# Expert tokens fetched from DRAM by row index, two pairs ahead, and RWKV units cut in three, in a two-layer hybrid network

## Chip, cores and metric

The kernel runs on one core of a Trainium2 chip: TensorE (PE) with its weight loads (PEld), VectorE (DVE), ScalarE (ACT), GpSimd (POOL), and SyncE (SP), whose queue issues nearly all transfers. The metric is the device time of one run in microseconds; the runs are of the whole program, both layers and the final norm.

## What is computed

Two streams of 256 tokens each, "latent" and "context", with 1024 channels go through two layers. A layer is a norm, one input projection, four token mixers of 256 channels (RWKV-7 and gated linear attention, both in two directions; window attention; S5), a gated sum of the four branches (the "merge"), an output projection, a second norm, and a mixture of 32 experts with 512 hidden channels. Layer 1 gives out only the latent stream. What the change touches is the experts and the RWKV mixer:

```python
def hier_moe(h, p):                       # n rows of 1024
    g_sel = argmax(hf @ p['w_router_g'] + p['b_router_g'])       # one of 4 groups
    e_logits = (hf @ p['w_router_e'] + ...)[rows, g_sel]         # its 8 experts
    top_v, top_i = lax.top_k(e_logits, TOP_K)                    # TOP_K = 2
    weights = softmax(top_v) * g_w[:, None]
...
    xb = h_pad[buf_tok].reshape(n_blk, MOE_BLOCK, d)             # rows sorted by expert
    def expert_block(args):
        x_blk, e = args
        hid = silu(x_blk @ p['w_exp_gate'][e]) * (x_blk @ p['w_exp_up'][e])
        return hid @ p['w_exp_down'][e]
    y_buf = lax.map(expert_block, (xb, blk_e)).reshape(cap, d) * buf_w[:, None]
    return segment_sum(y_buf, buf_tok, num_segments=n + 1)[:n]
```

The RWKV mixer is a linear recurrence over each stream, forwards and backwards, with a state of 64 x 64 per head; it is computed in chunks of 64 tokens, for which a triangular system is solved in each chunk.

## The kernel before

**Order of the work.** The program text gives the operations in one order; a scheduler places each in its engine's row by when its operands are due, and engines then run their own rows strictly in order. Layer 0 has 512 tokens in four tiles of 128 (`nt` = 4, `lo` = 0), layer 1 256 in two (`nt` = 2, `lo` = 256).

**RWKV units** (`rwkv_units`, L365). A layer has eight units: two halves of the channels (`hf`), two directions (`d`), two streams (`s`). `rwkv_sub` (L464) is one unit: it builds the tiles `ar`, `x`, `bk` and `sm` from decay and keys; writes the 16 x 16 diagonal blocks to DRAM (`ad`), reads them back in another layout (`lt`), solves them on VectorE in 15 steps of two small operations (`tm<-lt,ti`, `ti<-ti,tm`), and sends the inverses through DRAM (`td`) to `dc`; from these come `dT` and the state matmuls (psd, psw, pst, psta), which need the state of the unit before. `rwkv_pre` and `rwkv_half` prepare a direction and a half, `rwkv_finish` (L410) norms a half. Between these matmuls lie those of the merges: eight columns for each of four branches, 24 matmuls of 128x512 (128x256 in layer 1) a column (`pa<-hh,gs`, `pa<-hl,gs`).

**Second norm and routing** (`tail`, L1603). `norm2` norms a tile of 128 tokens to `h2` and, at its end, splits it in three bf16 parts `h2p` (24 KB of each partition in layer 0). `route` finds for each token and expert a position `posm` among that expert's tokens and the weight.

**Experts** (`moe`, L1642; `pair`, L1530). Sixteen pairs of experts, P0 to P15, 64 rows for each expert of a pair. A pair makes one-hot matrices `oh` of 128 tokens x 128 rows, and gathers with them on TensorE: `pg<-oh,h2p`, 8 blocks of channels x `nt` tiles x 3 parts, 96 bf16 matmuls in layer 0, 48 in layer 1, copied to `xT`. It transposes `oh` (pT, `oT`), gets the weights of the rows (pw, `ws`), multiplies gate and up (pgate and pup, 32 matmuls each), makes `hd` of them, transposes that (ph, `hT`), multiplies down (pd, 32), scales by `ws` in two parts `yp`, and puts the rows back to their tokens by matmul (`py<-yp,oT`, 4 x `nt`). Half of the py tiles are scaled and added to `x` by VectorE (`tm`), half by ScalarE and GpSimd (`ta`, three buffers). The gather of a later pair was placed by the scheduler among the matmuls of an earlier one.

**Weights.** A pair needs twelve loads of 1 MB, issued on SP's queue by `wtile` (L224) into a ring of slots: `EB` gives for each layer the tiles on the left and right side; with the four slots of the output projection's weights there are 13 in layer 0 and 15 in layer 1. A load waits for its slot to be read by TensorE's matmuls of the pair before.

A last loop (`overflow`) for experts with over 64 tokens runs no times with these inputs.

Of the kernel before, what the change touches and what calls it, by code (L numbers as in the profile page):

```python
# [9 lines left out]
F32 = mybir.dt.float32  # L10
# [10 lines left out]
D = 1024  # L21
# [3 lines left out]
EB = ((4, 5), (6, 5))  # L25
# [15 lines left out]
C_END = C_ROPE + 128  # L41
# [6 lines left out]
def _consts():  # L48
    c = np.zeros((128, C_END), np.float32)
    p = np.arange(128)  # L50
    c[:, C_ID:C_ID + 128] = np.eye(128)
    s = p % 64
    t = np.arange(64)
    c[:, C_MRW:C_MRW + 64] = s[:, None] < t
    c[:, C_MRW + 64:C_MRW + 128] = s[:, None] <= t
    c[:, C_MG:C_MG + 64] = s[:, None] <= t
    c[:, C_MG + 64:C_MG + 128] = s[:, None] >= t
    q = np.arange(128)
    c[:, C_MA:C_MA + 128] = np.where(q[None, :] <= p[:, None], 0.0, NEG)
# [10 lines left out]
    c[:, C_SEL:C_SEL + 12 * L] = r[:, None] == np.arange(12 * L)  # L70
    c[:, C_SLT:C_SLT + 128] = p[:, None] < p[None, :]
# [104 lines left out]
class Net:  # L176
# [186 lines left out]
    def rwkv_units(self, l, st, yT, p0, pool, depth):  # L363
        self.unit_tiles(st, p0, pool, depth)
        half, pre, sub, fin = self.rwkv_half, self.rwkv_pre, self.rwkv_sub, self.rwkv_finish  # L365
        na, u = st["first"]
        pp = st["pool"]
        for hf in range(2):
            y, nx = yT[:, hf, :], na
            for d in range(2):  # L370
                S = None
                for s in range(2):
                    if d and s and hf == 0:
                        nx = half(l, 1, st, pp)
                    S = sub(hf, d, s, u, S, st, na, y, pool)
                if d == 0:
                    u = pre(hf, 1, st, pp)
                elif hf == 0:
                    u = pre(1, 0, st, pp)
            fin(l, hf, st, y, pool)  # L380
            na = nx
# [28 lines left out]
    def rwkv_finish(self, l, hf, st, y, pool):  # L410
# [5 lines left out]
        ps = self.pc()  # L416
# [3 lines left out]
        s2 = st["pool"].tile([128, 512], F32, tag="pi", name="s2")[:, 0:nlo]  # L420
        self.act(s2, yc, AF.Square)
        ps = self.pc()
# [4 lines left out]
        ps = self.pc()  # L427
# [3 lines left out]
        ps = self.pc()  # L431
# [32 lines left out]
    def rwkv_sub(self, hf, d, s, u, S0, st, na, y, pool):  # L464

        nc = self.nc
        V, G = nc.vector, nc.gpsimd
        self.bt = f"B{s}"
        r, k_, v, lo = st["r"], st["k"], st["v"], st["lo"]
        pp, fo = u  # L470
        pp = pp[:, 4 * s:4 * s + 4, :]
        ident = self.ident
# [34 lines left out]
        ad = self.dr.tile([4, 2, 2, 32, 32], F32, name="ad", tag="ad", bufs=3)  # L507
# [5 lines left out]
        lt = st["p0"].tile([128, 16, 32], F32, tag="lt", bufs=2, name="lt")  # L513
        src = ad.rearrange("j e h s t -> (j e h) (s t)")
        dst = lt.rearrange("p s t -> p (s t)")
        for h in range(2):
            nc.sync.dma_start(dst[64 * h:64 * h + 64, 0:496],
                              src[:, None, 528 * h:528 * h + 496].to_broadcast([16, 4, 496]))
        ti = st["p0"].tile([128, 4, 16], F32, tag="ti", bufs=2, name="ti")
        V.tensor_copy(ti, self.cst[:, C_UN:C_UN + 64].rearrange("p (c t) -> p c t", c=4))  # L520
        tm = st["p0"].tile([128, 4, 16], F32, tag="tm", bufs=2, name="tm")
        for t in range(15):
            n = 15 - t
            self.tt(tm[:, :, 0:n], lt[:, None, t, t + 1:16].to_broadcast([128, 4, n]),
                    ti[:, :, t:t + 1].to_broadcast([128, 4, n]), OP.mult)
            self.tt(ti[:, :, t + 1:16], ti[:, :, t + 1:16], tm[:, :, 0:n], OP.add)
        td = self.dr.tile([128, 64], F32, name="td", tag="td", bufs=3)
        tv = td.rearrange("(q h g) f -> h q g f", h=2, g=4)
        for h in range(2):
            nc.sync.dma_start(tv[h], ti[64 * h:64 * h + 64].rearrange("p c t -> p (c t)"))  # L530
        dc = st["p0"].tile([128, 4, 16], F32, tag="dc", bufs=2, name="dc")
        nc.sync.dma_start(dc, td.rearrange("(j g) (c t) -> (g c) j t", j=4, t=16))
# [880 lines left out]
    def norm2(self, t, x, rw, lo, h2p, wr, lg, pool):  # L1413

        nc = self.nc
        V, G = nc.vector, nc.gpsimd
# [19 lines left out]
        self.split3([h2p[:, i, tl, :] for i in range(3)], h2, V)  # L1436
# [93 lines left out]
    def pair(self, wts, posv, wtv, h2p, x, mb, lo, pool, pooled=(1, 1, 1, 1)):  # L1530

        nc = self.nc
        V, G = nc.vector, nc.gpsimd
        nt = (512 - lo) // 128
        wg, wu, wd = wts
        p = self.onehot(posv, nt, pool, "oh", 2)
        pf = p.rearrange("p t e n -> p t (e n)")
        xT = pool.tile([128, 8, 128], F32, tag="xT", bufs=2, name="xT")
# [13 lines left out]
        V.tensor_copy(oT.rearrange("p t n -> p (t n)"), pT[:, 0:128 * nt])  # L1552
        pw = self.pc("pw")
        for t in range(nt):
            self.mm(pw[:, 0:6], pf[:, t, :], wtv[:, t], t == 0, t == nt - 1)
        ws = pool.tile([128, 1], F32, tag="ws", bufs=2, name="ws")
        for e in range(2):
            r = slice(64 * e, 64 * e + 64)
            V.tensor_reduce(ws[r], pw[r, 3 * e:3 * e + 3], AX.X, OP.add)
# [9 lines left out]
        self.tt(hd, hd, pu, OP.mult)  # L1569
# [15 lines left out]
        for n in range(2):  # L1585
            cs = slice(512 * n, 512 * n + 512)
            for t in range(nt):
# [10 lines left out]
                else:  # L1598
                    tm = pool.tile([128, 512], F32, tag="tm", bufs=2, name="tm")
                    self.tt(tm, ps, mb[s][:, cs], OP.mult)  # L1600
                    self.tt(xo, xo, tm, OP.add)

    def tail(self, l, lo, acc, rm, w):  # L1603
# [7 lines left out]
        st["h2p"] = h2p = rm.tile([128, 3, nt, D], BF, name="h2p")  # L1611
# [4 lines left out]
        with self.tc.tile_pool(name=f"rt{l}", bufs=1, reuse_waits="tile") as rp:  # L1616
# [13 lines left out]
            for t in range(lo // 128, 4):  # L1630
                self.project(t, w, acc, x, bs, lo, rp)
                self.norm2(t, x, rw, lo, h2p, wr, lg, rp)
# [9 lines left out]
    def moe(self, l, lo, st):  # L1642
        nc, io, x = self.nc, self.io, self.x
        posm, wt3, h2p, mb, plan, base = (st[n] for n in ("posm", "wt3", "h2p", "mb", "plan", "base"))
        banks = self.psum(f"pm{l}", G=2, A=2, B=2, C=2)
        self.bt = "B"
        with self.tc.tile_pool(name=f"ep{l}", bufs=1, reuse_waits="tile") as ep:
            for q in range(16):
                e0 = 2 * q
                wg, wu, wd = [[self.blocks([self.eload(l, 12 * q + 4 * i + 2 * h + e) for h in range(2)])  # L1650
                               for e in range(2)] for i in range(3)]
                posv = [posm[:, :, e0 + e:e0 + e + 1] for e in range(2)]
                wtv = wt3[:, :, e0:e0 + 2, :].rearrange("p t e i -> p t (e i)")
# [53 lines left out]
    def overflow(self, l, x, mb, lo, posm, wt3, plan, base, h2p, pool):  # L1707
# [7 lines left out]
        with tc.For_i(0, nv, 1) as b:  # L1715
# [16 lines left out]
            self.pair(w, [pe[:, i] for i in range(2)], wv.rearrange("p t e i -> p t (e i)"), h2p, x, mb, lo, pool)  # L1732
# [174 lines left out]
```

## Time and profile before

| | us |
|---|---|
| runs, lowest / median / highest of three | 2526.41 / 2531.51 / 2534.54 |
| the profiled execution | 2508.66 |
| its span | 2506.9 |
| TensorE busy | 2329.0 (93%) |
| VectorE busy | 1202.6 (48%) |
| ScalarE busy | 670.5 (27%) |
| GpSimd busy | 278.0 (11%) |
| gathers, `pg<-oh,h2p` x2304 | 163.2 busy |
| expert stage, layer 0 / layer 1 | 811 to 1401 / 2000 to 2496 |
| RWKV units, layer 0 / layer 1 | 341 to 585 / 1660 to 1895 |

The profile is of one execution. Busy times are of the engine's whole row; a stage's limits are read from the windows of that stage and from the waits that end last there. A row of the order of time gives start, duration, engine, line, operation, what is written and read, shapes and count; in brackets the idle time before it and what ended that.

### The profile page before, as it was taken

The numbers are of one execution on the slowest core, as the hardware profiler recorded it, in microseconds if no ns is written. First come the engines' busy times: TensorE is split into PE (matmuls) and PEld (weight loads), VectorE is DVE, ScalarE is ACT, GpSimd is POOL, SyncE is SP. The second block draws the span as 40 slices with busy tenths as digits, with TensorE's granted clock in tenths as the row PEclk, the third lists the DMA queues.
The fourth block names the chain that finished last, engine by engine and source line by source line (L and its number), as shares of the span: only waits on it lengthen the run. The fifth ranks groups of instructions, "written<-read, shape, count | busy, mean of one in ns | idle before, by whom it ended". The sixth has DMA issues, their size and how long they took to land. (4 is left out here: it accounts for less than half of the span.)

```text
span 2506.9 us, 42482 instructions
## 1 busy us (share of the span) xinstructions
PE 2329.0 (93%) x17303; PEld 1397.5 (56%) x17303; DVE 1202.6 (48%) x3267; ACT 670.5 (27%) x1229; POOL 278.0 (11%) x305
## 2 busy tenths in 40 slices
PE   5999999999998999999999799989899899999996
PEld 4867666677754445444443576767788444333332
DVE  6686666664435333222223678867665432222222
ACT  3254532323212111111111335543323211111111
POOL 0001000000000133132233100100000011111111
PEclk8999999999998999999999899989999899999999
DMA  6343021215723898787887254412227499999993
GB/s 242 121 146 95 29 64 45 73 43 191 263 70 151 339 389 339 309 334 309 350 315 319 74 169 148 131 56 56 90 63 281 154 417 418 401 397 396 396 409 157
DMA packets 143692, 548.23 MB, mean 219 GB/s; under 512 B 35028, under 2 KB 66132, under 8 KB 93060
## 3 DMA queue, kind: packets, MB, share of 16 engines
q1 hardware_dynamic: 138224, 539.51, 56.9%
q10 hardware_dynamic: 5268, 5.94, 0.7%
q8 instruction: 140, 2.29, 0.4%
q14 instruction: 60, 0.49, 0.1%
HBM read 541.78 MB, written 3.60 MB: 218 GB/s over the span
## 5 line engine op out<-in xcount | busy, mean ns | idle before, releaser
L270 PE MATMUL pa<-hh,gs 128*128 128x512 f32 (+2 forms) x1440 | 421.2, 366 | 10.2 <-ACT sg L273 6.1
L270 PEld LDWEIGHTS pa<-hh,gs 128*128 128x128 f32 (+1 forms) x1440 | 252.4, 188 | 69.8 <-issue 15.3
L270 PE MATMUL pd<-w,hT 128*64 128x512 f32 x1024 | 276.6, 599 | 13.1 <-ACT hT L273 12.4
L270 PE MATMUL pa<-hl,gs 128*128 128x512 f32 (+2 forms) x720 | 252.8, 363 | 0.0
L270 PE MATMUL pgate<-w,xT 128*64 128x512 f32 x1024 | 251.3, 596 | 0.0
L270 PE MATMUL pup<-w,xT 128*64 128x512 f32 x1024 | 249.2, 594 | 0.0
L276 POOL TENSOR_TENSOR ta<-ta,mb 128x512 f32<-128x512 f32 x93 | 127.1, 1373 | 1098.2 <-ACT ta L273 1098.2
L270 PEld LDWEIGHTS <-h2p 128*128 128x128 bf16 x2304 | 134.9, 99 | 78.0 <-issue 72.8
L270 PE MATMUL pg<-oh,h2p 128*128 128x128 bf16 x2304 | 163.2, 223 | 5.8 <-DVE nv L1686 4.2
L276 DVE TENSOR_TENSOR gs<-g,gs 128x1024 fp32r<-128x1024 f32 (+1 forms) x106 | 128.1, 1211 | 83.2 <-PE pa L270 56.7
L270 PEld LDWEIGHTS pd<-w,hT 128*64 128x64 f32 x1024 | 81.5, 136 | 146.7 <-issue 124.3
L273 ACT ACTIVATE gs<-g 128x1024 fp32r<-128x1024 f32 (+1 forms) x106 | 110.5, 1045 | 180.7 <-PE pa L270 139.1
L270 PEld LDWEIGHTS pup<-w,xT 128*64 128x64 f32 x1024 | 78.4, 137 | 143.1 <-issue 138.9
L270 PEld LDWEIGHTS pgate<-w,xT 128*64 128x64 f32 x1024 | 74.8, 137 | 139.6 <-issue 129.4
L270 PEld LDWEIGHTS pa<-hl,gs 128*128 128x128 f32 (+1 forms) x720 | 137.1, 190 | 27.3 <-issue 9.1
L270 PE MATMUL py<-yp,oT 128*128 128x512 f32 x384 | 133.1, 441 | 11.2 <-ACT ta L273 5.5
L286 DVE SCALAR_TENSOR_TENSOR hd<-hd,pgate 128x512 f32<-128x512 f32 x32 | 22.0, 688 | 246.7 <-ACT hd L273 246.7
L276 DVE TENSOR_TENSOR hd<-hd,pup 128x512 f32<-128x512 f32 x32 | 22.0, 688 | 218.0 <-PE pup L270 218.0
L276 POOL TENSOR_TENSOR x<-x,ta 128x512 f32<-128x512 f32 x93 | 122.7, 1326 | 4.9
L286 DVE SCALAR_TENSOR_TENSOR yp<-pd,ws,yp 128x512 fp32r<-128x512 f32 x64 | 47.8, 747 | 152.6 <-ACT yp L273 152.6
L273 ACT ACTIVATE yp<-pd,ws 128x512 fp32r<-128x512 f32 x64 | 44.1, 688 | 272.9 <-PE pd L270 272.9
L276 DVE TENSOR_TENSOR tm<-py,mb 128x512 f32<-128x512 f32 x99 | 66.7, 687 | 95.7 <-PE py L270 95.7
(499 smaller groups left out, 3427.1 us busy)
## 6 DMA issues: line engine op xcount, KB each, us to landing
w<-in_w_g SPq DMA_DIRECT2D x128, 1024.0 KB, 7.9
w<-in_w_d SPq DMA_DIRECT2D x128, 1024.0 KB, 10.5
w<-in_w_u SPq DMA_DIRECT2D x128, 1024.0 KB, 8.6
g<-in_w_ada SPq DMA_DIRECT2D x96, 512.0 KB, 4.0
g<-in_w_in_gate SPq DMA_DIRECT2D x64, 512.0 KB, 3.8
g<-in_w_in_rwkv SPq DMA_DIRECT2D x16, 512.0 KB, 3.6
wb<-in_w_branch SPq DMA_DIRECT2D x64, 128.0 KB, 3.1
w<-in_w_out SPq DMA_DIRECT2D x8, 1024.0 KB, 9.3
```

Source lines behind the costliest of these rows:

```text
L270: self.nc.tensor.matmul(out, lhsT, rhs, start=start, stop=stop, skip_group_check=True)
L273: self.nc.scalar.activation(out, in_, f, **kw)
L276: (eng or self.nc.vector).tensor_tensor(out, a, b, op)
L286: self.nc.vector.scalar_tensor_tensor(out, a, s, b, op0=op0, op1=op1)
```

## The change

The change has three parts.

1. **Experts.** `norm2` no longer splits `h2`; it writes it to DRAM (`h2d`, one transfer on SP for each tile). `pair` is cut: `seek(q)` makes the one-hot matrices, multiplies them with a column of token indices (`tid`) and with the weights (pw), turns the index into an integer (`ix`; rows without a token get one out of bounds) and issues on GpSimd's queue an indirect DMA that takes up to 128 rows of 4 KB from `h2d` to one of three buffers `xg`; rows out of bounds are skipped. `bring(q)` multiplies `xg` by 1 or 0 for rows with or without a token on VectorE, transposes it in eight fp32 blocks on TensorE, copies to `xT`, and makes `oT`. `seek` runs two pairs ahead, `bring` one; `bring`'s multiply is placed behind the pair's last `hd`. At a layer's start three memsets clear `xg`.
2. **Slots.** Two more in layer 0 (15), one more in layer 1 (16).
3. **RWKV units.** `rwkv_sub` becomes `rwkv_head`, `rwkv_solve` and `rwkv_rest`. In layer 0 (`depth` 3) head and solve go three units ahead of rest. In layer 1 (`depth` 4) one solve takes both streams' units: 4 solves of 30 VectorE operations instead of 8, each twice as wide. `rwkv_finish` uses another bank and a tile of its own.

```diff
-EB = ((4, 5), (6, 5))
+EB = ((4, 7), (7, 5))
...
+        nc.sync.dma_start(h2d[128 * tl:128 * tl + 128], h2)
...
-        self.split3([h2p[:, i, tl, :] for i in range(3)], h2, V)
...
+    def seek(self, posv, wtv, h2d, lo, pool):
...
+        p = self.onehot(posv, nt, pool, "oh", 3)
+        pf = p.rearrange("p t e n -> p t (e n)")
+        pw = self.pc("pw")
+        for t in range(nt):
+            self.mm(pw[:, 8:11], pf[:, t, :], self.tid[:, t], t == 0, t == nt - 1)
+        for t in range(nt):
+            self.mm(pw[:, 0:6], pf[:, t, :], wtv[:, t], t == 0, t == nt - 1)
...
+        V.tensor_copy(at[:, 0:3], pw[:, 8:11])
+        self.stt(ix, at[:, 0:1], 1024.0, at[:, 1:2], OP.add, OP.add)
...
+        nc.gpsimd.indirect_dma_start(xg, None, h2d, bass.IndirectOffsetOnAxis(ap=ix, axis=0),
+                                     bounds_check=128 * nt - 1, oob_is_err=False)
+    def bring(self, sent, lo, pool, after=None):
...
+        with self.tc.issue_after(after) if after is not None else nullcontext():
+            self.tsc(xg, xg, at[:, 2:3], OP.mult)
...
-                for t in range(nt):
-                    for i in range(3):
-                        self.mm(ps[:, 128 * kk:128 * kk + 128], h2p[:, i, t, 128 * k:128 * k + 128], pf[:, t, :],
-                                t == 0 and i == 0, t == nt - 1 and i == 2)
+                nc.tensor.transpose(ps[:, 128 * kk:128 * kk + 128], xg[:, 128 * k:128 * k + 128], self.ident)
...
+            sent = seek(0), seek(1)
+            got = self.bring(sent[0], lo, ep)
             for q in range(16):
...
+                sent = sent[1], seek(q + 2)
+                last = self.pair((wg, wu, wd), got, x, mb, lo, ep, (1, q < 15, 1, q < 15))
+                if q < 15:
+                    got = self.bring(sent[0], lo, ep, last)
```

```diff
+        if depth == 4:
+            cur = [head(0, s) for s in range(2)]
+            solve(cur)
+            ahead(1)
+            nxt = [head(1, s) for s in range(2)]
+            for i in range(4):
+                rest(cur[0])
+                if i < 3:
+                    solve(nxt)
+                rest(cur[1])
...
+        else:
...
+            go(0)
+            go(1)
+            ahead(1)
+            go(2)
+            for n in range(8):
+                rest(un[n])
+                if n in (1, 3):
+                    ahead(n // 2 + 2)
+                if n + 3 < 8:
+                    go(n + 3)
```

How the rows move, at three places (names: left of the arrow what is written, right what is read; buffer numbers behind an underscore).

TensorE in layer 0's experts, a late pair before, from the first gate matmul on; `h2p` is the stationary side of the gather:

```order
L270 MATMUL pgate<-w,xT 64x512
L270 MATMUL py<-yp,oT 128x512 x2
L270 LDWEIGHTS h2p
L270 MATMUL pg<-oh,h2p 128x128
...
L270 MATMUL py<-yp,oT 128x512 x4
...
L270 MATMUL pgate<-w,xT 64x512 x15
...
L270 MATMUL pup<-w,xT 64x512
```

The same place in the changed kernel, to the end of the pair:

```order
L272 MATMUL pgate<-w,xT 64x512
L272 MATMUL py<-yp,oT 128x512 x12
L272 MATMUL pgate<-w,xT 64x512 x15
L272 MATMUL pup<-w,xT 64x512 x16
L1663 MATMUL ph<-cst,hd 128x128 x4
...
L1635 MATMUL pg<-cst,xg_7792 128x128 x5
L272 MATMUL pd<-w,hT 64x512 x2
L1635 MATMUL pg<-cst,xg_7792 128x128 x2
L272 MATMUL pd<-w,hT 64x512 x7
L1635 MATMUL pg<-cst,xg_7792 128x128
...
L272 MATMUL pw<-tid,oh 128x3
```

The 96 gather matmuls between py, gate, up and down are gone; eight transposes of `xg` for the next pair, and the small matmuls with `tid` and the weights for a later one, stand behind ph and inside pd.

GpSimd in a late pair of layer 0's experts in the changed kernel; before, the row has the scalings and adds alone:

```order
L278 TENSOR_TENSOR ta<-ta,mb_7647 128x512
L278 TENSOR_TENSOR x_7263<-x_7263,ta 128x512
L278 TENSOR_TENSOR ta<-ta,mb_7647 128x512
L1619 DMA xg_7791<-h2d_7294,ix 128x1024
L278 TENSOR_TENSOR x_7265<-x_7265,ta 128x512
L278 TENSOR_TENSOR ta<-ta,mb_7656 128x512 x2
L278 TENSOR_TENSOR x_7267<-x_7267,ta 128x512
```

The indirect DMA stands between the second tile's scaling and its add, with two more tiles of the pair behind it.

VectorE in layer 1's RWKV units, at the start of a solve, before and in the changed kernel:

```order
L276 TENSOR_TENSOR tm<-lt,ti 128x4x15
L276 TENSOR_TENSOR ar_15166<-na,pp 128x4x64
L276 TENSOR_TENSOR ti<-ti,tm 128x4x15
L283 TENSOR_SCALAR sw<-ic,sp 128x512
L276 TENSOR_TENSOR tm<-lt,ti 128x4x14
```

```order
L278 TENSOR_TENSOR tm<-lt,ti 128x8x15
L278 TENSOR_TENSOR ic<-ic,pi 128x512
L278 TENSOR_TENSOR ti<-ti,tm 128x8x15
L278 TENSOR_TENSOR bk<-kv,sw 64x4x64
L278 TENSOR_TENSOR tm<-lt,ti 128x8x14
```

The steps still alternate with operations of the next units' heads, and each covers two units.

## Rows read from the trace of the kernel before

**Rows 1.** Windows: us, busy us (x instructions) by engine, clock, DMA share, GB/s.
```profile
990.00:1330.00 340.00, 327.98 (x2010) 143.99 (x2007) 79.44 (x142) 53.21 (x89) 90.13 (x70) 1.00 0.82 324
2010.00:2450.00 440.00, 422.54 (x2310) 169.76 (x2306) 102.20 (x189) 69.28 (x114) 73.76 (x56) 1.00 0.99 405
```

**Rows 2.** Waits of SyncE's queue, 990 to 1330 us: total us, times, longest.
```profile
SPq L224 <- PE pgate L270: 119.7, 33, 11.2
```

**Rows 3.** Order of time, TensorE, layer 0: start, us, engine, line, operation.
```profile
811.87 7.20 PE L270 MATMUL pg<-oh,h2p 128*128 128x128 bf16 x96 [2.31 <-DVE nv L1686]
...
819.30 3.23 PE L270 MATMUL pgate<-w,xT 128*64 128x512 f32 x14
...
851.62 7.09 PE L270 MATMUL pgate<-w,xT 128*64 128x512 f32 x32
```

**Rows 4.** Order of time, TensorE, layer 0, P8 and P9.
```profile
1100.76 1.07 PE L270 MATMUL pgate<-w,xT 128*64 128x512 f32 x2
...
1115.82 3.02 PE L270 MATMUL pg<-oh,h2p 128*128 128x128 bf16 x51
...
1141.31 1.07 PE L270 MATMUL pgate<-w,xT 128*64 128x512 f32 x2
```

**Rows 5.** Order of time, TensorE, layer 0, P14 and P15; idle time before in brackets.
```profile
1330.45 1.07 PE L270 MATMUL pgate<-w,xT 128*64 128x512 f32 x2
...
1332.70 1.40 PE L270 MATMUL py<-yp,oT 128*128 128x512 f32 x4 [0.51 <-DVE tm L276]
1334.84 1.19 PE L270 MATMUL py<-yp,oT 128*128 128x512 f32 x4 [0.75 <-ACT ta L273]
...
1351.72 0.66 PE L1572 MATMUL ph<-cst,hd 128*128 128x128 f32 x4 [0.78 <-DVE hd L276]
1352.21 0.39 PE L1550 MATMUL pT<-identb,oh 128*128 128x128 bf16 x4
1353.06 1.93 PE L270 MATMUL pd<-w,hT 128*64 128x512 f32 x4 [0.46 <-ACT hT L273]
...
1363.25 1.07 PE L270 MATMUL pgate<-w,xT 128*64 128x512 f32 x2
```

**Rows 6.** Order of time, TensorE, layer 1: P0, P1, P6, P7, P14, P15.
```profile
2000.42 7.09 PE L270 MATMUL pgate<-w,xT 128*64 128x512 f32 x32
...
2027.71 7.09 PE L270 MATMUL pgate<-w,xT 128*64 128x512 f32 x32
...
2179.70 1.07 PE L270 MATMUL pgate<-w,xT 128*64 128x512 f32 x2
...
2211.45 1.07 PE L270 MATMUL pgate<-w,xT 128*64 128x512 f32 x2
...
2433.04 1.07 PE L270 MATMUL pgate<-w,xT 128*64 128x512 f32 x2
...
2462.38 1.07 PE L270 MATMUL pgate<-w,xT 128*64 128x512 f32 x2
```

**Rows 7.** Order of time, VectorE, routing of layer 0.
```profile
803.86 1.23 DVE L276 TENSOR_TENSOR h2p<-h,h2p 128x1024 bf16<-128x1024 f32 x1 [0.63 <-ACT h2p L273]
```

**Rows 8.** Order of time, GpSimd, layer 0, P14.
```profile
1334.87 1.29 POOL L276 TENSOR_TENSOR ta<-ta,mb 128x512 f32<-128x512 f32 x1 [24.57 <-ACT ta L273]
1336.24 1.60 POOL L276 TENSOR_TENSOR x<-x,ta 128x512 f32<-128x512 f32 x1
```

**Rows 9.** Operations on tile xn: ns min/median/max, first and last start.
```profile
L281 DVE TENSOR_SCALAR xn<-x,n x2: 753/754/754, 1418.0 to 1418.7; 128x1024 f32<-128x1024 f32 x2
```

**Rows 10.** DMA issues: count, KB each, median us to landing.
```profile
out<-o SPq DMA_DIRECT2D x2, 512.0 KB, 2.6
```

**Rows 11.** Waits of TensorE, 341 to 585 us.
```profile
PE psc L270 <- DVE bk L276: 2.9, 2, 2.0
PE pc L270 <- DVE s L286: 2.2, 2, 1.9
```

**Rows 12.** Waits of TensorE, 1660 to 1895 us.
```profile
PE psc L270 <- DVE bk L276: 5.2, 3, 2.2
...
PE pc L270 <- ACT sq L273: 2.7, 1, 2.7
```

**Rows 13.** Windows, RWKV units of layer 1.
```profile
1660.00:1895.00 235.00, 221.92 (x2539) 175.48 (x2540) 159.32 (x534) 75.96 (x150) 1.82 (x5) 0.93 0.27 77
```

More of the change, by code (lines that the diff above doesn't have):

```diff
@@ L1 @@
 import math
-from contextlib import ExitStack
+from contextlib import ExitStack, nullcontext
 import numpy as np
@@ L364, in rwkv_units @@
         self.unit_tiles(st, p0, pool, depth)
-        half, pre, sub, fin = self.rwkv_half, self.rwkv_pre, self.rwkv_sub, self.rwkv_finish
+        pp = st["pool"]
+        sides = [(hf, d) for hf in range(2) for d in range(2)]
         na, u = st["first"]
[L367 to L381, printed above, removed]
+        nas, us, S = {0: na}, {(0, 0): u}, [None]
@@ new lines, in ahead, with solve, rest, head @@
+        def ahead(i):
+            hf, d = sides[i]
+            if hf not in nas:
+                nas[hf] = self.rwkv_half(l, hf, st, pp)
+            us[hf, d] = self.rwkv_pre(hf, d, st, pp)
+        def solve(v):
+            self.rwkv_solve(v, st)
+        def rest(w):
+            hf, d, s = w["at"]
+            S[0] = self.rwkv_rest(w, None if s == 0 else S[0], st, yT[:, hf, :], pool)
+        def head(i, s):
+            hf, d = sides[i]
+            return self.rwkv_head(hf, d, s, us[hf, d], st, nas[hf], pool)
@@ new lines, in rwkv_units, with go @@
+        if depth == 4:
[8 more added lines that the diff above has]
+                rest(cur[1])
+                if i == 2:
+                    self.rwkv_finish(l, 0, st, yT[:, 0, :], pool)
+                cur = nxt
+                if i < 2:
+                    ahead(i + 2)
+                    nxt = [head(i + 2, s) for s in range(2)]
+        else:
+            un = {}
+            def go(n):
+                un[n] = head(n // 2, n % 2)
+                solve([un[n]])
+            go(0)
[8 more added lines that the diff above has]
+                    go(n + 3)
+                if n == 4:
+                    self.rwkv_finish(l, 0, st, yT[:, 0, :], pool)
@@ L522, in rwkv_sub @@
         for t in range(15):
             n = 15 - t
[L524 to L530, printed above, removed]
@@ L533, in rwkv_sub, with rwkv_rest @@
+    def rwkv_rest(self, w, S0, st, y, pool):
+        nc = self.nc
+        V, G = nc.vector, nc.gpsimd
+        hf, d, s = w["at"]
+        self.bt = f"B{s}"
+        v, lo = st["v"], st["lo"]
+        ar, x, bk, sm, dc, pp = (w[n] for n in ("ar", "x", "bk", "sm", "dc", "pp"))
+        ident = self.ident
+        E = (slice(0, 64), slice(64, 128))
+        ts = slice(256 * s, 256 * s + 256)
+        outs = 256 * s >= lo
         dT = pool.tile([128, 4, 64], F32, tag="dT", name="dT")
@@ L1551, in pair @@
         oT = pool.tile([128, nt, 128], F32R, tag="oT", bufs=2, name="oT")
[L1552 to L1559, printed above, removed]
+        nc.vector.tensor_copy(oT.rearrange("p t n -> p (t n)"), pT[:, 0:128 * nt])
+        return xT, oT, ws
+    def pair(self, wts, got, x, mb, lo, pool, pooled=(1, 1, 1, 1)):
+        nc = self.nc
+        G = nc.gpsimd
+        nt = (512 - lo) // 128
+        wg, wu, wd = wts
+        xT, oT, ws = got
         pg, pu = self.pa("pgate"), self.pa("pup")
@@ L1568, in pair @@
         self.stt(hd, hd, 1.0, pg, OP.add, OP.mult)
-        self.tt(hd, hd, pu, OP.mult)
+        last = nc.vector.tensor_tensor(hd, hd, pu, OP.mult).ins
         ps = self.pc("ph")
@@ L1601, in pair @@
                     self.tt(xo, xo, tm, OP.add)
+        return last
     def tail(self, l, lo, acc, rm, w):
@@ L1610, in tail @@
         st["cnt"] = cnt = rm.tile([128, 32], F32, name="cnt")
-        st["h2p"] = h2p = rm.tile([128, 3, nt, D], BF, name="h2p")
+        st["h2d"] = h2d = self.dr.tile([128 * nt, D], F32, name=f"h2d{l}")
         nb = 4 * nt
@@ L1643, in moe @@
         nc, io, x = self.nc, self.io, self.x
-        posm, wt3, h2p, mb, plan, base = (st[n] for n in ("posm", "wt3", "h2p", "mb", "plan", "base"))
+        posm, wt3, h2d, mb, plan, base = (st[n] for n in ("posm", "wt3", "h2d", "mb", "plan", "base"))
         banks = self.psum(f"pm{l}", G=2, A=2, B=2, C=2)
@@ L1731, in overflow @@
                 V.tensor_copy(wv[:, :, i, :], wt3[:, :, bass.ds(e, 1), :].rearrange("p t o i -> p t (o i)"))
-            self.pair(w, [pe[:, i] for i in range(2)], wv.rearrange("p t e i -> p t (e i)"), h2p, x, mb, lo, pool)
+            sent = self.seek([pe[:, i] for i in range(2)], wv.rearrange("p t e i -> p t (e i)"), h2d, lo, pool)
+            self.pair(w, self.bring(sent, lo, pool), x, mb, lo, pool)
     def final(self, x, out, pool):
```

110 lines of the change are left out of this document (74 added, 36 removed).

## Prediction

> **What bounds the kernel now.** I read the busy time by stage first. In the steady part of the expert stage of layer 0 (990 to 1330 us) TensorE is busy 328 of 340 us and the DMA engines 82%; in layer 1's (2010 to 2450) TensorE is busy 423 of 440 and the DMA engines 99%, at 405 GB/s [rows 1]. Then the waits of the queue that issues the weights, in layer 0: what it waits for longest is a slot that TensorE has not yet read, 119.7 us behind the gate matmuls alone [rows 2]. So layer 0's experts are bound by TensorE, and in layer 1 TensorE and the weight transfers end almost together. Last I read TensorE's order of time, pair by pair. From the first pair's gate matmul (819.30) to the second's (851.62) are 32.3 us [rows 3]; from P8 to P9 in the middle, 40.55 us, in which one gather alone puts 51 matmuls of 0.059 us into the row [rows 4]; from P14 to P15, where nothing is left to gather, 32.80 us [rows 5]. In layer 1 the same three are 27.29, 31.75 and 29.34 us [rows 6]. In all, P0 to P15 takes 543.95 us in layer 0 and 461.96 us in layer 1. What the gather costs is therefore seen without a model: a late pair against one without it.
>
> **Part 1: the gather leaves TensorE.** A pair loses 96 bf16 matmuls in layer 0 and 48 in layer 1, at 3.02/51 = 0.059 us [rows 4], 5.7 and 2.8 us, and the breaks that they make in rows of other matmuls.
> *The first three pairs, layer 0.* These are interleaved with their neighbours as before. 32.3 - 5.7 = 26.6; but the gather matmuls stood in the waits that the pair without them shows: 0.51 and 0.75 (py), 0.78 (ph), 0.46 (pd) [rows 5], 2.5 us. I take 29.1 us each.
> *The other twelve.* The new row is that of the pair without a gather, 32.80, with eight fp32 transposes in it (the row behind the four of ph starts 0.49 us after them, so 0.12 each and 1.0 in all [rows 5]), four small matmuls with the token index, and two more breaks in pd. Five of the transposes stand where pd now waits 0.46 for hT, so about 0.4 is hidden; 0.6 is left of the transposes, 0.5 go to matmuls and breaks. 33.9 us each, bounds 32.8 and 35.
> Sum P0 to P15: 3 x 29.1 + 12 x 33.9 = 494.1, against 543.95: **-49.9 us**. The last pair has no gather before or after.
> *Layer 1.* 27.29 - 2.8 + 2.0 (the same waits without the 0.51) = 26.5, and 29.34 + 0.95 = 30.3: 3 x 26.5 + 12 x 30.3 = 443.1 against 461.96, -18.9. The weights nearly forbid it: a pair's are twelve loads of 1.05 MB, 12.58 MB, at the 405 GB/s of [rows 1] 31.1 us, and the gathered rows (about 32 of 4 KB, 0.13 MB) add 0.3. Sixteen loads lie in their slots at P0, so 14.7 pairs are still to come, 461 us to the last byte; that one is wanted by P15's down matmuls, some 22 us behind its gate as in [rows 5], so P15 cannot start before 439. 443.1 is 4 us above this floor: loads will be late here and there, and I take 3 us for it, **-16 us**, bounds 0 and -19.
> A page of the Trainium skill (SBUF — State Buffer, section "SBUF: two separate sides") puts a core's share of HBM at about 358 GB/s. By that a pair's weights would take 35.1 us, neither layer could go below it, and layer 1 would be slower than it is now; the 405 GB/s measured over 440 us speaks against it, and the row decides.
>
> **Part 2: the start of each expert stage.** Removed: the three-part split of the last token tile, which sits in VectorE's routing chain as 0.63 of wait and 1.23 of work [rows 7], 1.8 us; and the first gather, 7.20 us [rows 3], about 3.6 in layer 1. Added, in series: two index matmul groups and two small VectorE steps, 0.8; the gather. No DMA issued by GpSimd is in the trace. For its issue the nearest row is a GpSimd instruction, 1.29 us [rows 8] (the ends: nothing, and the 23 us of the last rival); for its landing the 512 KB output at 2.6 us [rows 10]. Then the masking multiply at 0.75, the size of xn [rows 9], eight transposes at half clock after the idle time, 2.0, and a copy, 0.6. Together 8.0, and some 2.3 us that a pair loses while TensorE climbs back. 819.30 - 1.8 - 7.2 + 8.0 + 2.3 = 820.6: **+1.3** in layer 0 and **+5** in layer 1. Bounds -3 and +10 each: with a landing of next to nothing, or one of 8 us.
> The three memsets lie on GpSimd beside the routing, the write of the tokens to DRAM lies on SP's queue ahead of the router; each is over while VectorE still routes.
>
> **Part 3: what is queued behind the gather later.** GpSimd in a late pair does four scalings and four adds at 1.29 to 1.60 us [rows 8], 10.8 us in layer 0 and half in layer 1; the gather stands between them. It is issued some 8 us into a pair, its rows are wanted in the next pair's down matmuls, so about 47 us of lead. The multiply is held back behind hd on VectorE, so it delays nothing that TensorE waits for, unless the gather is late. Cost taken: nothing, covered by 33.9 - 10.8 = 23.1 us of idle GpSimd.
>
> **Part 4: RWKV units.** The matmuls are the same; only their place changes. In 341 to 585 us TensorE waits 2.9 us for bk, and 2.2 for s [rows 11], with smaller ones some 8 us. With three units ahead I take half: **-4**, bounds +10 and -8. In layer 1 (1660 to 1895) it waits 5.2 us for bk and 2.7 for sq [rows 12], and the granted clock is 0.93 of full [rows 13], which at two levels is 14% of the 235 us at 1.2 GHz, up to 16 us lost. Solving two streams at once takes out 120 of 240 small VectorE steps. I take 5 of the waits and 5 of the clock: **-10**, bounds +10 and -25. In both layers merge columns are still being computed when the last unit ends, so the units' own chain sets no end: only holes in TensorE's row count.
>
> **Sum.** -49.9 + 1.3 - 16 + 5 - 4 - 10 = -73.6, say **-73**. The profiled execution, 2508.66, would be 2436. The runs' median, 2531.51, stands 0.9% above it; the difference carried over gives **2458 us**.
>
> **Rivals.**
> *Layer 1 stays with the weights* (0.15). For it: DMA at 99% [rows 1] already. Then pairs stay at 31.75 and the -16 goes: 2474.
> *The units gain more* (0.15): all waits and the slow clock go, -8 and -25, 2439.
> *Another bound appears in layer 0* (0.08). With the gather gone, a pair may wait for py's copies, or for the weights at 82% of DMA, or gathered rows that arrive late; at some 36.3 us, the mean of before, nothing of the -49.9 is left but 7: 2500. Against it: P14 to P15 [rows 5] has this very row and takes 32.80. If both layers' pairs stay, the whole change is within 0.3% or so, 0.02 of this.
> *The new unit order stalls TensorE* (0.05): +10 in each layer, 2492.
> *Slower: the gather holds GpSimd* (0.03). It issues 128 rows by an index, and the instruction may keep the engine until the descriptors of all are written. With a hold h a pair cannot be shorter than 10.8 + h in layer 0 and 5.4 + h in layer 1, since ta has three buffers, ScalarE's copies wait for them and TensorE's py for those. It decides from h = 23, and takes back all from about 26; at 30 pairs are 40.8 and 35.4 us, 15 x (40.8 - 36.3) + 15 x (35.4 - 30.8) + 6.3 - 14, +129: 2660. For it: no row prices it. Against: a GpSimd add beside VectorE grows from 1.29 to 1.60 us only [rows 8], and it would take twenty times an instruction of this engine.
> The same page and section of the Trainium skill has the rule that speaks for it: a DMA from GpSimd cannot write its descriptors while a VectorE operation holds the port that the two share, and one of 0.62 us became 3.1 beside a copy. By that figure a gather would be held some 3 us, and only one that meets such an operation again and again would come to 23.
>
> **How the numbers follow.** The forecast has 0.54, its own range 2445 to 2472 by the bounds of parts 2 and 4. The range to hold 8 in 10 takes in the rivals with 0.15 on both sides, and half of those at 2492 and 2500: **2428 to 2498**. About 0.3% (7.6 us) is what a measurement of this kernel tells from no change: faster 0.95, same 0.02, slower 0.03.
>
> **What would show it.** In the profile after: no pg<-oh,h2p; P8 to P9 near 33.9 with no wait of pg for xg; P0 within a few us of 820; layer 1 from P0 to P15 near 446 with DMA still at 0.99; GpSimd's gather issue under 5 us; psc's wait for bk smaller in both unit stages. It is wrong if TensorE waits for xg in each pair, if GpSimd's share in the expert stages exceeds two thirds, if a late pair stays above 36 us, or if the unit stages grow.

## The result, and the profile after

| | before | after |
|---|---|---|
| runs of the first comparison, median (us) | 2533.03 (2526.41 to 2537.51, 4) | 2437.92 (2435.60 to 2439.97, 4) |
| span of the profiled execution | 2506.9 | 2434.5 |
| TensorE busy | 2329.0 | 2233.6 |
| GpSimd busy | 278.0 | 316.0 |

The ratio is 0.9649, 95% interval 0.9604 to 0.9693, which is between 100 and 78 us less; the two medians stand 95 us apart. 2458 was forecast, with 2428 to 2498. The sign and the mechanism hold; by the medians the gain is about 22 us larger than the sum of the steps. Three later runs of the kernel before, of 2545 to 2550 us, count as slow and stay out of the ratios.

The two profiles alone show 72 us, almost the forecast, and that is a coincidence: the first profile of the kernel before met less half clock ahead of 365 us than most of its executions. A second one (e1 below) has a span of 2532.2. The stages stand as follows, read from the starts of TensorE's rows ("P0" and "P15" as ahead of the prediction; "output projection" is its first matmul `pa<-w,acc`):

| stage (us) | before, first profile | before, second | after | foreseen |
|---|---|---|---|---|
| start to output projection, layer 0 | 714.13 | 734.10 | 730.39 | -4 |
| from there to P0 | 105.17 | 106.23 | 107.46 | +1.3 |
| P0 to P15, layer 0 | 543.95 | 543.90 | 487.06 | -49.9 |
| P15 to output projection, layer 1 | 577.12 | 581.35 | 559.78 | -10 |
| from there to P0 | 60.05 | 60.24 | 63.27 | +5 |
| P0 to P15, layer 1 | 461.96 | 461.95 | 440.49 | -16 |
| P15 to the end of the span | 44.5 | 44.4 | 46.1 | 0 |

From the second profile to the changed kernel's the differences add up to -97.7. P0 to P15 repeats within 0.1 us in the two profiles of before; what moves between executions of one program are the stages in which TensorE is at half clock (1.2 GHz) for a part.

The steady windows of the expert stages, in the changed kernel (columns as in [rows 1]):

```profile
960.00:1320.00 360.00, 335.71 (x1453) 124.01 (x1453) 122.69 (x199) 62.84 (x107) 123.40 (x98) 1.00 0.95 385
2010.00:2380.00 370.00, 351.62 (x1513) 125.31 (x1511) 98.46 (x188) 60.08 (x99) 75.15 (x60) 1.00 1.01 419
```

In layer 0 TensorE is busy 336 of 360 us and the transfers have risen from 82% to 95%; in layer 1 they are at 1.01 with 419 GB/s, where [rows 1] had 405. What SyncE's queue waits for in layer 1, before (2010 to 2450 us) and in the changed kernel (2010 to 2380), in all, times, longest; and what TensorE waits for in the latter:

```profile
SPq L224 <- PE pgate L270: 150.0, 45, 8.3
```
```profile
SPq L226 <- DMA w<-in_w_g: 100.9, 48, 3.1
SPq L226 <- PE pgate L272: 28.0, 20, 3.7
```
```profile
PE ph L1663 <- DVE hd L1660: 10.2, 13, 0.8
PE py L272 <- ACT ta L275: 8.2, 11, 0.7
```

Before, the queue waited for slots that TensorE had not read; now it waits mostly for loads to land, and TensorE waits for no load. A late pair of layer 0 on TensorE, changed kernel, in order of time:

```profile
1089.84 1.07 PE L272 MATMUL pgate<-w,xT 128*64 128x512 f32 x2
...
1092.09 1.39 PE L272 MATMUL py<-yp,oT 128*128 128x512 f32 x4 [0.51 <-DVE tm L278]
1094.23 1.20 PE L272 MATMUL py<-yp,oT 128*128 128x512 f32 x4 [0.75 <-ACT ta L275]
...
1111.11 0.66 PE L1663 MATMUL ph<-cst,hd 128*128 128x128 f32 x4 [0.78 <-DVE hd L1660]
1111.60 0.33 PE L1639 MATMUL pT<-identb,oh 128*128 128x128 bf16 x3
1111.77 0.77 PE L1635 MATMUL pg<-cst,xg 128*128 128x128 f32 x5
1112.47 1.93 PE L272 MATMUL pd<-w,hT 128*64 128x512 f32 x4
1114.33 0.44 PE L1635 MATMUL pg<-cst,xg 128*128 128x128 f32 x2
...
1118.28 0.33 PE L1635 MATMUL pg<-cst,xg 128*128 128x128 f32 x1
...
1118.50 0.24 PE L272 MATMUL pw<-tid,oh 128*128 128x3 bf16 x4
...
1123.47 1.07 PE L272 MATMUL pgate<-w,xT 128*64 128x512 f32 x2
```

1123.47 - 1089.84 = 33.63 us, for the 40.55 of [rows 4] (before, late pairs of 40.6 take turns with pairs of 36.1 to 36.4; now all take 33.5 to 33.6). It is the pair without a gather of [rows 5], with its waits of 0.51, 0.75 and 0.78, and with the transposes `pg<-cst,xg` in it. The wait of 0.46 ahead of pd is gone: five transposes fill it. No pg waits for `xg`. GpSimd in the same pair:

```profile
1095.62 1.60 POOL L278 TENSOR_TENSOR x<-x,ta 128x512 f32<-128x512 f32 x1
1097.19 1.27 POOL L278 TENSOR_TENSOR ta<-ta,mb 128x512 f32<-128x512 f32 x1
1098.60 1.03 POOL L1619 DMA_INDIRECT xg<-h2d,ix  x1 [0.15 <-issue]
1099.66 1.28 POOL L278 TENSOR_TENSOR x<-x,ta 128x512 f32<-128x512 f32 x1
```

The gather holds GpSimd for 1.03 us and the next add follows at once. And the start of layer 0's experts on TensorE:

```profile
829.24 0.26 PE L272 MATMUL pw<-tid,oh 128*128 128x3 bf16 x4 [4.01 <-DVE tid L1746]
...
835.95 1.97 PE L1635 MATMUL pg<-cst,xg 128*128 128x128 f32 x8 [4.74 <-DVE xg L283]
837.85 1.98 PE L272 MATMUL pgate<-w,xT 128*64 128x512 f32 x4
```

It waits 4.01 us for the routing's and the one-hot matrices' rows on VectorE, of which `tid` came last, and 4.74 for the first gather with its multiply; then eight transposes take 1.97.

### The profile page after: what moved, and what is told of

Read it like the earlier page. It is cut to its first block, busy times and chain, and to the rows that moved or that the text cites. A ratio compares the mean times of both kernels' runs of the same rounds, so it can differ in the third digit from the quotient of the medians.

```text
span 2434.5 us, 38729 instructions
## 1 busy us (share of the span) xinstructions
PE 2233.6 (92%) x15351; PEld 1302.5 (54%) x15351; DVE 1220.8 (50%) x3229; ACT 657.7 (27%) x1217; POOL 316.0 (13%) x351
## 5 line engine op out<-in xcount | busy, mean ns | idle before, releaser
L272 PE MATMUL pgate<-w,xT 128*64 128x512 f32 x1024 | 262.6, 602 | 0.0
L272 PEld LDWEIGHTS py<-yp,oT 128*128 128x128 f32 x384 | 62.1, 190 | 122.2 <-ACT ta L275 44.5
L272 PE MATMUL pa<-gs,hh 128*128 128x256 f32 x480 | 107.6, 319 | 2.4 <-DVE gs L278 1.8
L275 ACT ACTIVATE yp<-pd,at 128x512 fp32r<-128x512 f32 x64 | 44.0, 688 | 241.7 <-PE pd L272 241.7
L288 DVE SCALAR_TENSOR_TENSOR yp<-pd,at,yp 128x512 fp32r<-128x512 f32 x64 | 47.7, 745 | 122.6 <-ACT yp L275 122.6
```

The lines of the kernel that those rows point to most:

```text
L272: self.nc.tensor.matmul(out, lhsT, rhs, start=start, stop=stop, skip_group_check=True)
L275: self.nc.scalar.activation(out, in_, f, **kw)
L288: self.nc.vector.scalar_tensor_tensor(out, a, s, b, op0=op0, op1=op1)
```

## The experiments

**e1, e2: both kernels again, for a second profile.** No edit.

> The kernel before, unchanged, for a second profile. Its four runs stand at 2526 to 2538 us, its profiled execution at 2509; the changed kernel's runs and its profile agree (2436). Theory A (the first profile met less half clock than most executions): the second profile's own time is 2520 to 2540, with the same rows in the same order, and stretches of half clock where the first has none, above all between 185 and 365 us. Rival B (a profiled execution of this kernel is faster than an unprofiled one): the second profile is again near 2509 while its unprofiled run is near 2532.

> The changed kernel, unchanged, for a second profile. Theory A (where half clock falls before 450 us is chance of an execution): the second profile has the half-clock stretches of 184 to 204, 222 to 236, 330 to 363 us partly elsewhere or not at all, and its span is 2410 to 2440, shorter by what is missing. Rival C (the changed rows cause them): they stand at the same places within 2 us and the span is 2434 within 3.

Measured: e1 2534.03 us, span 2532.2; e2 2437.09, span 2435.3. For the kernel before, first and second profile, the windows of 150 to 250 and 250 to 370 us, and then the changed kernel's (the last column but two is the granted clock):

```profile
150.00:250.00 100.00, 93.86 (x937) 70.03 (x938) 72.89 (x171) 44.95 (x94) 7.16 (x24) 0.93 0.33 101
250.00:370.00 120.00, 111.83 (x830) 79.66 (x829) 81.25 (x275) 54.48 (x129) 0.44 (x2) 1.00 0.17 50
```
```profile
150.00:250.00 100.00, 93.64 (x897) 67.91 (x898) 66.80 (x165) 41.14 (x88) 6.25 (x19) 0.83 0.31 94
250.00:370.00 120.00, 112.40 (x586) 80.09 (x585) 73.60 (x237) 52.36 (x124) 1.43 (x6) 0.91 0.16 46
```
```profile
150.00:250.00 100.00, 93.62 (x900) 67.79 (x901) 67.14 (x166) 41.61 (x90) 6.24 (x19) 0.85 0.30 94
250.00:370.00 120.00, 112.40 (x587) 80.03 (x586) 74.13 (x239) 52.29 (x124) 1.43 (x6) 0.91 0.15 46
```

The same program is granted 0.93 and 1.00 in one execution, 0.83 and 0.91 in the next, with TensorE busy as long in both, for fewer matmuls; the changed kernel's first profile had 0.85 and 0.91. Theory A holds for e1. In e2 the stretches are again at 182 to 204, 222 to 238 and 332 to 368, as C said; but they are also in the second profile of the kernel before, so the changed rows don't cause them, and e5 shows the changed kernel without most of them.

**e3: the experts' part alone.** The change's parts 1 and 2 on the kernel before, with the old units.

```diff
-EB = ((4, 5), (6, 5))
+EB = ((4, 7), (7, 5))
...
-        self.split3([h2p[:, i, tl, :] for i in range(3)], h2, V)
...
+            sent = seek(0), seek(1)
+            got = self.bring(sent[0], lo, ep)
```

> The kernel before with the experts' part of the change and the slots, and the RWKV units as they were. Theory A (the gather is nearly all of it): layer 0 from P0 to P15 487 us, layer 1 440 us, 78 less than before in the two, starts some 5 later in all: 2450 to 2462. Rival D (the units bring about as much as the experts do not explain, 95 - 73): 2460 to 2470. Rival E (the experts are all): 2438.

Measured: 2458.15 us (2434.40 to 2470.15, 6 runs), ratio 0.9728, interval 0.9669 to 0.9787, beside runs of the kernel before with a median of 2518.18. P0 to P15 are 487.23 and 440.65 us, as in the changed kernel; layer 1 from the last py of layer 0 to the output projection 546.06, as before (539.13 and 543.83). The experts' part is worth 60 us beside these runs, the whole change (e2's one run) 81. E falls. The median lies in A's range, 2 us below D's, but with runs from 2434 to 2470 A and D can't be told apart by time; A's stages are met.

**e4: the units' part alone.** The change's part 3 on the kernel before.

```diff
-                    S = sub(hf, d, s, u, S, st, na, y, pool)
...
+            for n in range(8):
+                rest(un[n])
```

> The kernel before with the RWKV units' part of the change alone; gather by matmul and the slots as they were. Theory A: 8 to 18 us less than before, 2514 to 2525, the expert stages as before (544 and 462 us from P0 to P15). Rival D: 20 to 25 less, 2508 to 2513. Rival F (the units' order brings nothing, or costs, since TensorE was 97% busy there): 2528 to 2540.

Measured: 2509.57 us (2488.70 to 2523.48, 12 runs), ratio 0.9967, interval 0.9937 to 0.9997; P0 to P15 543.69 and 461.94, as before. Its profile has the early clock of the first profile of before and a span of 2486.9, 20.0 less than it. Windows from layer 1's first psc to its output projection, the kernel before, and e4:

```profile
1634.00:1940.00 306.00, 288.19 (x2958) 227.48 (x2957) 197.05 (x625) 105.98 (x214) 1.82 (x5) 0.93 0.34 110
```
```profile
1633.00:1920.00 287.00, 272.04 (x2962) 217.18 (x2961) 186.50 (x501) 106.55 (x216) 1.82 (x5) 0.96 0.37 119
```

The same matmuls (2958 and 2962 records) keep TensorE busy 288.19 and 272.04 us: 16 of the 19 us are busy time, at a granted clock of 0.93 and 0.96, and 3 are idle time. The ranges of time expected were laid from 2532; beside these runs, with a median of 2518, only differences count. By the runs the gain is 8.6 us (0.8 to 15.9 by the interval), as A has it; by this one profile it is 20, as D has it. F falls, though by the interval alone only just.

**e5: the changed kernel, timed beside more runs.** No edit.

> The changed kernel, timed beside more runs of the kernel before. In profiles with half clock at the same places before 450 us the two stand 97 us apart; in the first profile of the kernel before, with less of it there, 72. Theory A (both kernels fall into either pattern by chance of an execution): ratio 0.962 to 0.970, and the runs of this kernel spread over some 25 us as those of the kernel before do (2507 to 2550). Rival C (the changed kernel has one pattern only): its runs stay within 2435 to 2445, and the ratio goes with the runs of the kernel before alone.

Measured: 2433.08 us (2428.14 to 2437.89, 6 runs) beside 2532.91 (2510.95 to 2549.92, 11 runs); ratio 0.9636, interval 0.9596 to 0.9675. Its profile has the clock of the first profile of before ahead of 365 us (first psc at 272.31, there 270.86, in the changed kernel's first profile 279.34), so it meets both, and C falls in that; but its eleven runs of three comparisons lie within 2428 to 2440, and A's spread of 25 us isn't there. What is won early is lost later in that execution: layer 1 from the last py to the output projection is 529.0 in e5, 521.2 in the first profile. Why the kernel before spreads over 31 us (2507 to 2538, by the runs that are in the ratios) and the changed one over 12 stays open.

**e6: single solves in layer 1.**

```diff
-            solve(cur)
+            for w in cur:
+                solve([w])
...
-                    solve(nxt)
+                    for w in nxt:
+                        solve([w])
...
-            w["dc"] = dc = st["p0"].tile([128, 4, 16], F32, tag="dc", bufs=st["depth"] if m == 2 else 3, name="dc")
+            w["dc"] = dc = st["p0"].tile([128, 4, 16], F32, tag="dc", bufs=st["depth"], name="dc")
```

> The changed kernel with eight single solves in layer 1 in place of four joint ones, in the same skewed order. Theory G (the skewed order brings the 23 us of layer 1's units): layer 1 from the last py of layer 0 to the output projection within 5 us of the changed kernel's 521, time +0 to +5. Rival H (the joint solve brings them, since VectorE's 240 small steps stand in the row ahead of what TensorE waits for): that stretch is 10 to 20 longer, as is the time, and the half clock near 1690 and 1810 us is back.

Measured: 2439.06 us (2428.55 to 2442.17, 6 runs), ratio 0.9642, interval 0.9601 to 0.9684: 6 us more than e5, within both intervals. From the last py of layer 0 to the output projection 529.2 us; eight profiles with the joint solve give 517.0 to 530.8, three with the old units 539.1, 543.8 and 546.1. 529.2 lies between G's bound of 526 and H's of 531, so neither has the number. It is within the range of the joint solve and 10 us below the old units, so the skewed order brings most of it, as G says; what the joint solve adds, up to some 6 us, is below what these runs tell. One wait does show it: the first psc to wait for bk waits 3.59 us here, and 1.1 in e5 and the other seven profiles with the joint solve. The row in this run, then in e5:

```profile
1648.07 1.35 PE L272 MATMUL psc<-ar,bk 64*128 64x192 f32 x5 [3.59 <-DVE bk L278]
```
```profile
1632.27 2.19 PE L272 MATMUL psc<-ar,bk 64*128 64x192 f32 x8 [1.11 <-DVE bk L278]
```

H's half clock is not back where it stood: this profile has 7 us of it near 1813 us, but 217 us behind the first psc, where the kernel before has its own 175 behind; and e5, with the joint solve, has 20 us of it near 1675 and 1700.

**e7: py pinned between the next pair's gate matmuls.**

```diff
+        ahead = nxt(last) if nxt else None
...
+                with self.tc.issue_after(g) if g is not None else nullcontext():
...
+                if n * nt + t in stops:
+                    g = self.gate(png, pwg, pxT, stops[n * nt + t], m)
```

> The changed kernel with the py matmuls of each pair chained between the next pair's gate matmuls (6 py, 6 gate, 4 py, 4 gate, 4 py, 4 gate, 2 py, the rest), as the first three pairs have them, for all pairs. Theory I (layer 0's late pairs take 33.6 and not 29.7 us because of py's waits and breaks alone): late pairs 30 to 31 us, now held by the weights (12.8 MB at 419 GB/s are 30.6), P0 to P15 in layer 0 455 to 465 in place of 487, layer 1 unchanged at 440; 25 to 32 us faster than the changed kernel. Rival J (the weights' slots come free no sooner): TensorE waits for weights in the middle of gate or up, pairs stay above 33, time within 8 us of the changed kernel.

Measured: 2407.70 us (2391.12 to 2409.50, 6 runs), ratio 0.9528, interval 0.9488 to 0.9569: 25 us less than the changed kernel beside the same runs, and 125 less than before. Late pairs take 31.5 us in layer 0 and 29.2 in layer 1; P0 to P15 464.9 and 433.8. A late pair on TensorE in e7, then its steady windows:

```profile
1098.56 0.73 PE L1695 MATMUL py<-yp,oT 128*128 128x512 f32 x2 [0.32 <-DVE tm L278]
1099.23 2.80 PE L1648 MATMUL pgate<-w,xT 128*64 128x512 f32 x12
1101.95 1.20 PE L1695 MATMUL py<-yp,oT 128*128 128x512 f32 x4
1103.08 1.94 PE L1648 MATMUL pgate<-w,xT 128*64 128x512 f32 x8
...
1117.36 0.66 PE L1670 MATMUL ph<-cst,hd 128*128 128x128 f32 x4 [0.82 <-DVE hd L1667]
...
1130.74 0.65 PE L1648 MATMUL pgate<-w,xT 128*64 128x512 f32 x2
```
```profile
940.00:1280.00 340.00, 327.53 (x1458) 122.10 (x1458) 110.27 (x209) 65.46 (x109) 120.46 (x98) 1.00 1.01 413
1960.00:2330.00 370.00, 351.50 (x1541) 128.44 (x1539) 102.21 (x195) 62.37 (x101) 83.97 (x64) 1.00 1.01 419
```

Of the waits at py one of 0.32 us is left in the pair; 0.82 ahead of ph stays. Theory I holds in the time and in P0 to P15, with a pair half a microsecond above its range. That the weights now hold the pair isn't shown for layer 0: the transfers are at 1.01, but TensorE waits for no load there (8.9 us at ph and 3.5 at py are all its waits from 940 to 1280), so 31.5 is still its own row. Layer 1 was expected unchanged, and that failed: its late pairs go from 30.1 to 29.2, below the 30.0 that 12.58 MB take at 419 GB/s, by eating the loads that lie ready, until TensorE waits 1.4 us for weights in the last pairs.

**e8: the old slots.**

```diff
-EB = ((4, 7), (7, 5))
+EB = ((4, 5), (6, 5))
```

> The changed kernel with 13 and 15 slots for the weights as before. Theory K (layer 0 is bound by TensorE's row, layer 1 by the transfers): P0 to P15 in layer 0 487 within 2, in layer 1 442 to 445 since one load of 1.05 MB less lies ready. Rival L (the slots are part of the gain): layer 0 5 to 15 longer, late pairs above 34.

Measured: 2429.81 us, P0 to P15 490.24 and 441.17, late pairs 33.6 and 30.1. Layer 0 is 3.2 us longer, in the third and fourth pair (31.0 and 33.6 in place of 29.7 and 31.3): with the two more slots the scheduler keeps the better row for one more pair, and in neither does TensorE wait for a load. L falls. K's 2 us were too tight, and its 442 to 445 for layer 1 was missed: 441.17 is 0.7 above the changed kernel, with pairs of 30.08 in both. A stage held by the transfers would end some 2.5 us later with one load less in hand (1.05 MB at 419 GB/s); so in layer 1, too, a pair is TensorE's row, and the transfers just keep up.

**e9: each gather twice.** One line doubled.

```diff
+        nc.gpsimd.indirect_dma_start(xg, None, h2d, bass.IndirectOffsetOnAxis(ap=ix, axis=0),
+                                     bounds_check=128 * nt - 1, oob_is_err=False)
```

> The changed kernel with every gather issued twice into the same buffer; the second issue waits on GpSimd until the first has landed, some 8 us. Theory M (GpSimd has over 20 us free in a pair, the rival of a held GpSimd decides only from 23): late pairs 33.6 in layer 0 within 0.3, layer 1 30.1 to 30.5 for the extra 0.13 MB a pair, starts 2 to 5 us later in each layer, in all 2436 to 2448. Rival N (what stands behind the gather on GpSimd is already near the path): late pairs of layer 0 rise by 4 to 9 us, 2480 to 2560.

Measured: 2447.51 us, late pairs 33.6 and 30.1, from the output projection to P0 112.4 in layer 0 (107.5) and 67.1 in layer 1 (63.3). GpSimd's waits for the second issue, in all; the end of a late pair of layer 0 on GpSimd, and of one of layer 1; and two late pairs of layer 0 on TensorE:

```profile
POOL xg L1621 <- DMA xg<-h2d,ix: 108.4, 29, 7.5
```
```profile
1076.20 2.50 POOL L278 TENSOR_TENSOR x<-x,ta 128x512 f32<-128x512 f32 x2
1079.80 1.03 POOL L1621 DMA_INDIRECT xg<-h2d,ix  x1 [1.09 <-DMA xg<-h2d,ix]
1100.71 1.28 POOL L278 TENSOR_TENSOR ta<-ta,mb 128x512 f32<-128x512 f32 x1 [19.88 <-ACT ta L275]
```
```profile
2112.06 1.01 POOL L1621 DMA_INDIRECT xg<-h2d,ix  x1 [6.40 <-DMA xg<-h2d,ix]
2129.14 1.54 POOL L278 TENSOR_TENSOR ta<-ta,mb 128x512 f32<-128x512 f32 x1 [16.07 <-ACT ta L275]
```
```profile
1062.67 1.07 PE L272 MATMUL pgate<-w,xT 128*64 128x512 f32 x2
...
1096.28 1.07 PE L272 MATMUL pgate<-w,xT 128*64 128x512 f32 x2
```

M's numbers are met, but not by the hold that it describes. The scheduler put the second issue behind the pair's last add. In layer 0's late pairs it waits only 0.5 to 1.7 us there, in layer 1 up to 7.5, and GpSimd then stands idle for another 15 to 20 us. The longer hold falls into idle time and no scaling or add waits for it. So a second gather costs the pairs nothing, but N, a long hold ahead of the pair's scalings and adds, is not tested.

**e10: no gather.** The same lines taken out.

> The changed kernel without the indirect transfers: the experts compute with rows of zeros, all else is as it was. Theory M: late pairs of layer 0 33.6 as before, since the gather is hidden; each stage's start 3 to 5 us earlier (the first gather's landing); layer 1 from P0 to P15 438 to 441; 6 to 12 us less in all. Rival O (the gather's 4 KB rows disturb the weights' transfers): layer 0 pairs below 33, layer 1 pairs at 29.5 or less.

Measured: 2431.26 us; late pairs 33.6 and 30.1; output projection to P0 103.1 and 59.8, 4.4 and 3.5 less than in the changed kernel; P0 to P15 488.0 and 440.4. M holds in the pairs and the starts, and O falls: the 4 KB rows cost what their first landing costs, nothing in the pairs. M's 6 to 12 us in all can't be told from one run, since the changed kernel's own eleven lie between 2428 and 2440.

## Why the prediction was right, and too small

**What bounds, and part 1, layer 0.** Right: TensorE's row, and the pair without a gather as its price. 33.63 came for 33.9, since the five transposes fill all of the 0.46 (0.83 net, not 1.1), nine times, and 33.5 twice; the fourth pair still has the better row (31.3), which I had counted with the late ones; the first three take 26.8, 29.7 and 29.7 for 29.1 each. 56.8 us, not 49.9.

**Part 1, layer 1.** The step that failed is "loads will be late here and there, and I take 3 us for it": TensorE waits for no load in the changed kernel's layer 1, and a late pair takes 30.1 (30.3 foreseen). -21.5 came, beyond the bound of -19. Behind it stands "at the 405 GB/s ... P15 cannot start before 439": I took the rate of a stage in which the queue waited on TensorE for a limit. Asked faster, the transfers gave 419, 30.0 us for a pair's weights. The changed kernel's 440.5 still lies above that floor, but e7's 433.8 lies below it. The 419 GB/s hold over 370 us, on a program that runs on one core. The Trainium skill (SBUF — State Buffer, section "SBUF: two separate sides") gives about 358 GB/s from HBM to a core, as half of what a stack gives to two cores. By these rows that share was no limit here.

**Part 2.** Foreseen +1.3 and +5, measured +1.2 to +2.3 and +3.0 to +3.2. The gather's place in it: in layer 0 4.4 us by e10 and e9's 4.9 for a second one, in layer 1 3.5 and 3.8, where issue and landing were put at 3.9. The 2.3 us for a first pair "while TensorE climbs back" name no row, and the first pair is not longer by them: P0 to P1 takes 26.8 us, less than any pair behind it.

**Part 3 and the slower rival.** A gather holds GpSimd 1.0 us, for the 1.29 taken; its landing takes 7.9 us in the median, for the 2.6 taken, in a lead of 47 us. All gathers of the changed kernel, by their tile:

```profile
L1619 POOL DMA_INDIRECT xg<-h2d,ix x32: 990/1034/1197, 830.9 to 2335.2; - x32
...
DMA to landing us min/median/max: 3.4/7.9/9.4
```

At 7.9 us beside the weights the lead is still some six times enough. The rival asked for 23 us of hold, and it falls by the hold itself, 1.20 us at the longest, and by e10, whose pairs without a gather are as long; what a long hold ahead of the adds would cost no run shows. What the Trainium skill (SBUF — State Buffer, the same section) says of a GpSimd DMA shut out by VectorE no run here shows: the longest issue is 1.20 us.

**Part 4.** Layer 0: -4 foreseen; -3.7 against the second profile. But e4, e5 and e7, with the early clock of the first profile, reach layer 0's output projection at 716, 718 and 716 us for its 714, so a gain in layer 0 isn't shown. Layer 1 is the term that was mis-sized: "5 of the waits and 5 of the clock". From the last py on, the stretch is 19 us shorter in the mean over all profiles (eight of 517.0 to 530.8, mean 524.1; three of the old units, mean 543.0); from the first psc on, where the units' new order begins, it is 15 (286 to 300, mean 292, for 306 to 308). In e4 idle time gave 3 us and busy time 16. By the granted clocks of its two windows the half clock took some 21 us before (0.07 of 306) and 11 in e4 (0.04 of 287), so about 10 of the 16 are the clock's, twice what I took; what the other 6 are stays open.

The kernel before shows the two side by side, in TensorE's order of time and in the windows:

```profile
1808.00 4.78 PE L270 MATMUL psc<-ar,bk 64*128 64x192 f32 x16 [2.17 <-DVE bk L276]
1814.61 2.16 PE L270 MATMUL psc<-ar,bk 64*128 64x192 f32 x8 [1.83 <-DVE bk L276]
```
```profile
1790.00:1808.00 18.00, 14.67 (x90) 11.73 (x91) 13.31 (x48) 6.46 (x12) 0.00 (x0) 1.00 0.43 141
1808.00:1824.00 16.00, 14.17 (x84) 11.71 (x84) 12.60 (x57) 2.64 (x10) 0.00 (x0) 0.57 0.17 38
```

psc waits 2.17 us for bk, and 1.83 a little later; ahead of that the granted clock is full, and from there to 1824 it is 0.57. All three profiles of the old units have this stretch, some 174 us behind the first psc, and in none of the nine with the new order is there half clock from 131 to 216 us behind it. Another stands at 1686 behind a wait of 1.21, for 14 us. That the waits bring the stretches about is not shown, and the length of a wait doesn't tell what follows. A wait of 2.28 us shortly before has full clock behind it, up to 1808:

```profile
1782.34 0.39 PE L270 MATMUL pa<-hh,gs 128*128 128x256 f32 x1 [2.28 <-ACT sg L273]
```

In the new order the two waits for bk that are left (1.11 and 1.93 us in e4) have from 3 us of half clock behind them, in e4 (1690 to 1696 at a clock of 0.72), to 14, in e5 (1632 to 1646 at 0.52). In e5 it also stands from 1673 and from 1697 with no wait of TensorE over 0.7 us since 1639. No run changed one of these waits by itself; what brings half clock in these stages stays open.

**The sum.** Measured terms: -3.7 + 1.2 - 56.8 - 21.6 + 3.0 - 21.5 + 1.7 = -97.7 against the second profile, for -73: the experts' two stages gave 12 more than foreseen, the stages with the units 11 more. The rival "the units gain more" had the number, 2439, but not this cause. Carrying a difference of stages to the runs' median was right; taking the first profile's 0.967 of clock for the kernel's own was not, it merely did no harm. And "7.6 us" for what a measurement tells was too small: the runs of the kernel before spread over 31.

## What to carry to other kernels

Where a stage has one period without the work that a change removes, that period, with what the change puts into it, is the forecast; here it was right to 1% for a late pair. A transfer rate read in a stage that isn't bound by transfers is no limit. A stage that loses waits can win more than the waits: in e4 it won 3 us of idle time and 16 of busy time, some 10 of them by the clock; but the half clock behind one and the same wait ran from 3 to 14 us between executions, so no price for a wait came out of these runs. And look where a probe lands in the row before reading it: in e9 the scheduler put the second gather where it held nothing up.

## What the runs showed of the hardware

An indirect DMA of up to 128 rows of 4 KB costs GpSimd 1.0 us (1.20 at most) and lands in 3.4 to 9.4 us, 7.9 in the median. The same program is granted half clock at different places in different executions: two profiles of the kernel before differ by 25 us of span, with about 165 and 206 us at half clock (summed over windows of 2 us). The transfers hold 419 GB/s over 370 us, with a gather of rows on another queue beside them.
